# Banded attention in a hybrid mixer block: scores in passes of full height, values with the probabilities stationary

## The chip, the core and the metric

The kernel runs on one core of one Trainium2 chip. The metric is the device time of one execution in microseconds. A profile of one execution gives every instruction's start and duration on the engines: TensorE (PE for matmuls, PEld for the loads of the stationary operand), VectorE (DVE), ScalarE (ACT), GpSimd (POOL) and the DMA queue of SyncE (SP).

## What is computed

The reference is one layer of a decoder block with five token mixers (A to E) over 1024 positions of width 1024. One projection feeds all five; each branch is gated by SiLU(z), projected back, weighted by a sigmoid gate and summed. The change concerns branch C alone, sliding-window attention with 8 query heads, 2 key/value heads, head size 64, a window of 128, a relative bias and learned sinks:

```python
def _swa_sinks(q, k, v, sinks, band_bias):
    ...
    kb, vb = band(k), band(v)          # block n sees blocks n-1 and n: 256 keys
    s = jnp.einsum('bniKgd,bnjKd->bnKgij', qb, kb).astype(jnp.float32) * (hd ** -0.5)
    s = s + band_bias.astype(jnp.float32).reshape(1, 1, HKV, G, W, 2 * W)
    ...
    m = jnp.maximum(jnp.max(s, axis=-1, keepdims=True), sink)
    p = jnp.exp(s - m)
    p = p / (jnp.sum(p, axis=-1, keepdims=True) + jnp.exp(sink - m))
    o = jnp.einsum('bnKgij,bnjKd->bniKgd', p.astype(v.dtype), vb)
    return o.reshape(B, S, HQ, hd)
```

## The kernel before

Almost all of the kernel's time goes into large projections. A projection unit loads 128 columns of weights (512 KB), splits them into a high part `wh` (rounded by ACT, L222) and a low part `wl` (the rest, by GpSimd, L223), and runs 48 matmuls of 512 columns in threes, high x high, high x low, low x high (`mm3`, L277 to L279). These are the background matmuls of this text.

The branches' own work is written as Python generators. Each `tick()` in a projection unit, after every second k, so after six background matmuls, resumes the generators of the moment for one step. That sets the order in which instructions are emitted; a scheduler then orders them on each engine, and each engine runs its list strictly in order.

`attn_c` is such a generator. It runs under `m_units(3)`, twelve units of two gates and one branch projection in turn, and ends in the units of `z_units("cz", ...)`, whose `finish` needs the branch's output. It has 32 tasks: 8 blocks of 128 queries (`n`), two key/value heads (`g`), two pairs of query heads (`ip`). Step `i` of its loop has three parts with a tick between each: the scores of task i (`scores`), the values of task i-2 if it closes a head group (`values`), the transposes of task i-1 (`trans`).

- `split(n)` cuts the queries of a block: the 64 rows of the own half of `q` hold the rounded queries (ACT, L1394), the other 64 rows the rest (DVE, L1395). `ck_fn` does the same for the keys: `kk[g]` holds the rounded keys in both halves, `kl` the rest.
- `scores`: per head one matmul on all 128 rows (L1406), which gives (rounded + rest of q) x rounded k, and one on the 64 rows of one half (L1407), rounded q x rest of k. DVE scales and adds the bias out of PSUM (L1411), takes the maximum (L1414 to L1417); ACT makes exp and the row sums (L1419, L1421); DVE adds, inverts (L1422, L1423) and multiplies the probabilities with the inverse (L1425).
- `trans`: the probabilities are transposed on TensorE (L1437) and copied out of PSUM by ACT as `pT` (L1438).
- `values`: the values are the stationary operand, 128 keys x 64, and `pT` with 512 columns (4 heads x 128 queries) moves past it (L1448). The output stands with the head's 64 channels in partitions, each `g` in its half. ACT copies it to `yC` (L1451).

PSUM has two tiles of 512 columns for scores (`pa`), two (`pb`) for transposes and values, and two double ones (`mm`) for the background. The queries have three buffers, `p` two, `pT` one.

The branch projection of a unit ends in a product on DVE (L1029, out of PSUM) and a sum on GpSimd into `merged` (L1032).

Of the kernel before, what the change touches and what calls it, by code (L numbers as in the profile page):

```python
# [9 lines left out]
F32 = mybir.dt.float32  # L10
F32R = mybir.dt.float32r
AF = mybir.ActivationFunctionType
ALU = mybir.AluOpType
# [3 lines left out]
P = 128  # L17
T = 1024
# [113 lines left out]
def trunk(ctx, tc, a, out):  # L132
    nc = tc.nc
    act, dve, pool, pe, sp = nc.scalar, nc.vector, nc.gpsimd, nc.tensor, nc.sync

    def dump(name, ap):
        if name in a:
            sp.dma_start(a[name], ap)

    def open_pool(name, side="left", **kw):  # L140
        st = ExitStack()
        pl = st.enter_context(tc.tile_pool(name=name, bufs=1, side=side, reuse_waits="tile", **kw))
        return pl, st
# [11 lines left out]
    def nm(s):  # L155
        uid[0] += 1
        return f"{s}_{uid[0]}"

    def mm_t():
        return psm.tile([P, 2, 512], F32, name=nm("mm"), tag="mm")  # L160
# [17 lines left out]
    def pa_t():  # L178
        return pss["a"][0].tile([P, 512], F32, name=nm("pa"), tag="pa")

    def pb_t():
        return pss["b"][0].tile([P, 512], F32, name=nm("pb"), tag="pb")
# [8 lines left out]
    def bcol(*key):  # L191
        return col("b_in", _TIDX[key])

    ident = cst.tile([P, P], F32, name="ident")
# [23 lines left out]
    def f32(ap):  # L218
        return ap.bitcast(F32)
# [131 lines left out]
    def project(hi, lo):  # L351
        ps = mm_t()
        for hf in range(2):
            tl = slice(hf * 512, hf * 512 + 512)
            for k in range(8):
                wl_ = slice(k * P, (k + 1) * P)
                mm3(ps[:, hf, :], hi[:, wl_], lo[:, wl_], hTh[k][:, tl], hTl[k][:, tl], k == 0, k == 7)
                if k % 2:
                    tick()
        return ps  # L360

    units = []
    pools = {}
# [209 lines left out]
    def wait(n):  # L573
        for _ in range(n):
            yield
# [762 lines left out]
    def open_c():  # L1338
        st_["pd"].close()
        pc_, st_["pc"] = open_pool("pc", side="right")  # L1340
        pools["pc"] = pc_
        pools["yC"] = pc_.tile([P, 4, T], F32, name="yC")
        band = pc_.tile([P, 8, 256], F32, name="band")
        sp.dma_start(band, pools["band_src"])
        pools["band"] = band
        dump("dbg_band", band)
        pools["kk"] = [pc_.tile([P, T], F32R, name=f"kk{g}") for g in range(2)]
        pools["kl"] = pc_.tile([P, T], F32R, name="kl")
        pools["vt"] = pc_.tile([P, 8, P], F32, name="vt")
    ev(open_c)  # L1350

    def ck_fn(hi, lo):
        ps = project(hi, lo).rearrange("p a b -> p (a b)")
        b = bcol("ck", 0)

        for g in range(2):
            own, oth = slice(64 * g, 64 * g + 64), slice(64 - 64 * g, 128 - 64 * g)
            kk = pools["kk"][g]
            act.activation(kk[own], ps[own], AF.Identity, bias=b[own])
            dve.scalar_tensor_tensor(out=pools["kl"][own], in0=ps[own], scalar=b[own], in1=f32(kk[own]),  # L1360
                                     op0=ALU.add, op1=ALU.subtract)
            dve.tensor_copy(kk[oth], f32(kk[own]))

    def cv_fn(hi, lo):
        ps = project(hi, lo).rearrange("p a b -> p (a b)")
# [12 lines left out]

    def attn_c():
        pl = pools["pc"]  # L1380
        y, kk, kl, vt, band = (pools[k] for k in ("yC", "kk", "kl", "vt", "band"))
        tasks = [(n, g, ip) for n in range(8) for g in range(2) for ip in range(2)]
        qs, pts, pp, pos = {}, {}, {}, {}

        def dims(n):
            nk = 2 if n else 1
            return nk, ((n - 1) * P if n else 0), nk * P

        def split(n):
            for g in range(2):  # L1390
                q = pl.tile([P, 4, P], F32R, name=nm("q"), tag="q", bufs=3)
                own, oth = slice(64 * g, 64 * g + 64), slice(64 - 64 * g, 128 - 64 * g)
                src = y[own, :, n * P:(n + 1) * P]
                act.activation(q[own], src, AF.Copy)  # L1394
                dve.tensor_tensor(out=q[oth], in0=src, in1=f32(q[own]), op=ALU.subtract)  # L1395
                qs[n, g] = q

        def scores(n, g, ip):
            nk, k0, w = dims(n)
            q = qs[n, g]  # L1400
            r = slice(64 * g, 64 * g + 64)
            ps = pa_t()
            s3 = ps.rearrange("p (t m) -> p t m", t=2)[:, :, 0:w]
            for e in range(2):
                i = 2 * ip + e
                pe.matmul(s3[:, e, :], q[:, i, :], kk[g][:, k0:k0 + w], start=True, stop=False)  # L1406
                pe.matmul(s3[:, e, :], q[r, i, :], kl[r, k0:k0 + w], start=False, stop=True)  # L1407
            h0 = 4 * g + 2 * ip
            p = pl.tile([P, 2, 256], F32, name=nm("p"), tag="p", bufs=2)
            pv_ = p[:, :, 0:w]  # L1410
            dve.scalar_tensor_tensor(out=pv_, in0=s3, scalar=0.125, in1=band[:, h0:h0 + 2, 256 - w:256],  # L1411
                                     op0=ALU.mult, op1=ALU.add)
            mx = pl.tile([P, 8], F32, name=nm("mx"), tag="mx", bufs=4)
            dve.tensor_reduce(mx[:, 0:2], pv_, axis=AX.X, op=ALU.max)  # L1414
            dve.tensor_tensor(out=mx[:, 0:2], in0=mx[:, 0:2], in1=sinks[:, h0:h0 + 2], op=ALU.max)
            dve.tensor_tensor(out=mx[:, 2:4], in0=sinks[:, h0:h0 + 2], in1=mx[:, 0:2], op=ALU.subtract)
            dve.tensor_scalar_mul(mx[:, 0:2], mx[:, 0:2], -1.0)  # L1417
            for e in range(2):
                act.activation(pv_[:, e, :], pv_[:, e, :], AF.Exp, bias=mx[:, e:e + 1],  # L1419
                               accum_out=mx[:, 4 + e:5 + e])  # L1420
            act.activation(mx[:, 2:4], mx[:, 2:4], AF.Exp)  # L1421
            dve.tensor_tensor(out=mx[:, 4:6], in0=mx[:, 4:6], in1=mx[:, 2:4], op=ALU.add)  # L1422
            dve.reciprocal(mx[:, 4:6], mx[:, 4:6])  # L1423
            for e in range(2):
                dve.tensor_scalar_mul(pv_[:, e, :], pv_[:, e, :], mx[:, 4 + e:5 + e])  # L1425
            pp[n, g, ip] = p

        def trans(n, g, ip):
            nk, k0, w = dims(n)
            p = pp.pop((n, g, ip))  # L1430
            if ip == 0:
                pts[n, g] = pl.tile([P, 2, 512], F32, name=nm("pT"), tag="pT", bufs=1)
            pt = pb_t()
            pt4 = pt.rearrange("p (m t c) -> p m t c", m=2, t=2)
            for e in range(2):
                for m in range(nk):
                    pe.transpose(pt4[:, m, e, :], p[:, e, m * P:(m + 1) * P], ident)  # L1437
            act.activation(pts[n, g][:, 0:nk, ip * 256:ip * 256 + 256],  # L1438
                           pt.rearrange("p (m x) -> p m x", m=2)[:, 0:nk, :], AF.Copy)

        def values(n, g):
            nk, k0, w = dims(n)
            r = slice(64 * g, 64 * g + 64)
            if g == 0:
                pos[n] = pb_t()
            po = pos[n]
            for m in range(nk):
                pe.matmul(po[r, :], vt[:, k0 // P + m, r], pts[n, g][:, m, :], start=(m == 0), stop=(m == nk - 1),  # L1448
                          tile_position=(0, 64 * g))
            if g:  # L1450
                act.activation(y[:, :, n * P:(n + 1) * P], po.rearrange("p (i c) -> p i c", i=4), AF.Copy)  # L1451

        split(0)
        yield from wait(4)
        N = len(tasks)
        for i in range(N + 2):
            if i < N:
                scores(*tasks[i])
                if i % 4 == 1 and i + 3 < N:
                    split(tasks[i][0] + 1)  # L1460
            yield
            if i >= 2 and tasks[i - 2][2]:
                values(*tasks[i - 2][:2])
            yield
            if 1 <= i <= N:
                trans(*tasks[i - 1])
            yield
        marks.add("yC")
        dump("dbg_yC", y)

    start_bg("c", attn_c, 1.0)
    m_units(3, False)
    z_units("cz", 2, lambda t: pools["yC"][:, t, :], lambda t: "yC" in marks, "c")
# [51 lines left out]
    for t in range(8):  # L1525
# [6 lines left out]
        if t < 7:  # L1532
            ps = mm_t()
# [12 lines left out]
        n = len(parts)  # L1546
        for i, part in enumerate(parts):
            p, c0, w = part
# [42 lines left out]
```

## Time and profile before

| | us |
|---|---|
| median of 3 runs | 1709.17 (1707.18 to 1710.69) |
| the profiled execution | 1703.68 |
| its span, first to last instruction | 1701.9 |

| group in the attention stage (1204 to 1445 us) | count | busy us |
|---|---|---|
| background matmuls L277 to L279 | 609 | 262.2 summed |
| L1406, score pass on 128 rows (256 wide) | 56 | 15.7 |
| L1407, score pass on 64 rows (256 wide) | 56 | 21.3 |
| L1437, transposes of the probabilities | 120 | 32.5 |
| L1448, values, two records for each matmul | 60 | 34.8 |

The spans of matmuls overlap in the profile, so the busy times of the groups add up to more than the stage. What a matmul costs is read from the distance between starts. A row of the timeline reads: start in us, duration in us, engine, line, operation, output<-inputs by the program's names, tile shapes, count; and, in brackets, the idle time of the engine ahead of it with what ended that. A row of the groups reads: line, engine, operation, output<-inputs, shapes, count | busy us, mean ns of one | idle us just before them, and what ended it. `64*128` names the part of the array that a matmul uses: 64 rows, 128 columns.

### The profile page before, as it was taken

What the parts mean: (1) busy time and instruction counts of PE and PEld (TensorE: products, weight loads), DVE (VectorE), ACT (ScalarE), POOL (GpSimd) and SP (SyncE); (2) the same over time, 40 slices, a digit from 0 to 9 for tenths busy, and PEclk for the clock granted to TensorE, in tenths of its full rate; (3) what the DMA queues carried; (4) which work ended last, traced back from release to release, by engine and by line L of the source; (5) the groups of instructions that cost most, each with busy time, mean ns of one, the idle gap of its engine ahead of it and who ended that gap; (6) DMA issues with size and microseconds to landing.
All of it is one profiled execution on the core that took longest, in us unless ns stands there. A gap on an engine that the chain in (4) does not pass through costs nothing.

```text
span 1701.9 us, 18997 instructions
## 1 busy us (share of the span) xinstructions
PE 1644.6 (97%) x7634; PEld 1305.6 (77%) x7634; DVE 843.4 (50%) x1299; ACT 647.8 (38%) x1055; POOL 596.7 (35%) x315
## 2 busy tenths in 40 slices
PE   8989699999999998999999999999999999999998
PEld 7568588879788877888888777888765655888877
DVE  6678743485999873244546442210355544001712
ACT  6343223523421133435553566222544543212311
POOL 1454322432522249323344456552122212621121
PEclk9899799999999999999999999999999999999999
DMA  4111001110111111131111111121100001112322
GB/s 159 39 56 59 25 32 38 38 37 14 38 50 50 50 38 50 62 124 38 38 38 52 48 39 49 50 74 42 45 25 26 25 25 38 38 50 75 111 89 85
DMA packets 27128, 87.49 MB, mean 51 GB/s; under 512 B 5104, under 2 KB 6560, under 8 KB 26912
## 3 DMA queue, kind: packets, MB, share of 16 engines
q1 hardware_dynamic: 26896, 86.15, 15.8%
q8 instruction: 60, 0.98, 0.2%
q14 instruction: 28, 0.23, 0.0%
q10 hardware_dynamic: 144, 0.13, 0.0%
HBM read 82.06 MB, written 5.78 MB: 52 GB/s over the span
## 4 chain that ended last, share of the span: by engine, by line
PE 80%; DVE 13%; ACT 3%; POOL 2%; issue 1%; DMA 0%; SPq 0%; DVEq 0%; ACTq 0%; POOLq 0%
PE mm L278 22%; PE mm L277 22%; PE mm L279 22%; DVE qk L484 2%; PE pb L1448 2%; DVE lt L692 2%; DVE Ad L694 1%; PE pa L1407 1%; DVE v L484 1%; PE pb L722 1%; PE pa L722 1%; DVE m L612 1%; PE pb L1437 1%; PE pa L664 1%; DVE p L1183 1%
## 5 line engine op out<-in xcount | busy, mean ns | idle before, releaser
L277 PE MATMUL mm<-hTh,wh 128*128 128x512 f32 x1472 | 599.1, 407 | 0.0
L279 PE MATMUL mm<-hTh,wl 128*128 128x512 f32 x1472 | 588.3, 400 | 10.8 <-POOL wl L223 10.8
L278 PE MATMUL mm<-hTl,wh 128*128 128x512 f32 x1472 | 594.6, 404 | 0.0
L223 POOL TENSOR_TENSOR wl<-raw,wh 128x1024 fp32r<-128x1024 f32 x113 | 276.4, 2446 | 679.6 <-ACT wh L222 679.2
L277 PEld LDWEIGHTS mm<-hTh,wh 128*128 128x128 f32 x1472 | 279.3, 190 | 71.5 <-issue 10.8
L279 PEld LDWEIGHTS mm<-hTh,wl 128*128 128x128 f32 x1472 | 279.2, 190 | 69.5 <-POOL wl L223 12.0
L278 PEld LDWEIGHTS mm<-hTl,wh 128*128 128x128 f32 x1472 | 279.5, 190 | 68.4 <-issue 13.6
L222 ACT ACTIVATE wh<-raw 128x1024 fp32r<-128x1024 f32 (+1 forms) x131 | 129.9, 998 | 392.9 <-issue 237.7
L876 DVE SCALAR_TENSOR_TENSOR pc<-u,sm,pc 128x1024 f32<-128x1024 f32 x120 | 154.6, 1289 | 3.8
L277 PE MATMUL mm<-yh,wh 128*128 128x512 f32 x320 | 129.0, 403 | 0.0
L278 PE MATMUL mm<-yl,wh 128*128 128x512 f32 x320 | 128.8, 402 | 0.0
L279 PE MATMUL mm<-yh,wl 128*128 128x512 f32 x320 | 126.2, 395 | 0.0
L972 DVE SCALAR_TENSOR_TENSOR sg<-mm,sm,sg 128x1024 f32<-128x1024 f32 x20 | 25.7, 1283 | 126.6 <-ACT sg L971 100.8
L1032 POOL TENSOR_TENSOR merged<-merged,sg 128x1024 f32<-128x1024 f32 x24 | 58.9, 2455 | 58.7 <-DVE sg L1029 36.3
L277 PEld LDWEIGHTS mm<-yh,wh 128*128 128x128 f32 x320 | 60.1, 188 | 18.4 <-issue 3.2
L278 PEld LDWEIGHTS mm<-yl,wh 128*128 128x128 f32 x320 | 60.1, 188 | 17.1 <-issue 3.9
L279 PEld LDWEIGHTS mm<-yh,wl 128*128 128x128 f32 x320 | 60.1, 188 | 12.7
L1029 DVE TENSOR_TENSOR sg<-mm,sg 128x1024 f32<-128x1024 f32 x27 | 33.0, 1220 | 51.8 <-PE mm L279 34.2
L223 DVE TENSOR_TENSOR wol<-raw,woh 128x1024 fp32r<-128x1024 f32 x8 | 10.1, 1265 | 90.1 <-ACT woh L222 89.9
L1564 POOL TENSOR_TENSOR res<-res,xr 128x512 f32<-128x512 f32 x14 | 17.8, 1292 | 83.8 <-DVE res L1562 76.0
L1411 DVE SCALAR_TENSOR_TENSOR p<-pa,band 128x512 f32<-128x512 f32 (+1 forms) x32 | 21.0, 658 | 48.2 <-PE pa L1407 48.1
L279 PE MATMUL mm<-woh,ml 128*128 128x512 f32 x112 | 44.3, 395 | 0.0
(426 smaller groups left out, 2389.2 us busy)
## 6 DMA issues: line engine op xcount, KB each, us to landing
raw<-in_w_t SPq DMA_DIRECT2D x94, 512.0 KB, 3.5
raw<-in_w_br SPq DMA_DIRECT2D x20, 512.0 KB, 3.5
xt<-in_x SPq DMA_DIRECT2D x8, 512.0 KB, 8.7
raw<-in_w_mem SPq DMA_DIRECT2D x8, 512.0 KB, 3.6
raw<-in_w_out SPq DMA_DIRECT2D x8, 512.0 KB, 3.5
xr<-in_x SPq DMA_DIRECT2D x8, 512.0 KB, 5.1
out_dram<-res SPq DMA_DIRECT2D x7, 512.0 KB, 2.9
d_rt<-d_rb SPq DMA_DIRECT2D x1, 1536.0 KB, 8.0
```

The source lines that it names most:

```text
L222: act.activation(hi, raw, AF.Copy)
L223: eng.tensor_tensor(out=lo, in0=raw, in1=f32(hi), op=ALU.subtract)
L277: pe.matmul(o, lh, rh, start=start, stop=False)
L278: pe.matmul(o, lh, rl, start=False, stop=False)
L279: pe.matmul(o, ll, rh, start=False, stop=stop)
L484: dve.scalar_tensor_tensor(out=acc, in0=xp[:, j:j + 1024], scalar=cw(j), in1=acc, op0=ALU.mult, op1=ALU.add)
L692: dve.tensor_tensor(out=t3, in0=V3[:, 0:r, j:j + 1].broadcast_to([P, r, n]), in1=A3[:, j:j + 1, j + 1:32].broadcast_to([P, r, n]), op=ALU. ...
L722: pe.matmul(ps[:, j * P:(j + 1) * P], lhs[:, j, :], rhs[:, j, :], start=True, stop=True)
L876: dve.scalar_tensor_tensor(out=acc, in0=u[:, j:j + 1024], scalar=w(j), in1=acc, op0=ALU.mult, op1=ALU.add)
L1029: dve.tensor_tensor(out=(merged[d] if first else sgs[d])[:, cl], in0=p2, in1=sgs[d][:, cl], op=ALU.mult)
L1032: (dve if last else pool).tensor_tensor(out=merged[d][:, cl], in0=merged[d][:, cl], in1=sgs[d][:, cl], op=ALU.add)
L1448: pe.matmul(po[r, :], vt[:, k0 // P + m, r], pts[n, g][:, m, :], start=(m == 0), stop=(m == nk - 1), tile_position=(0, 64 * g))
```

## The change

Three things are done differently in `attn_c` and `ck_fn`.

The keys: `kk[g]` holds the rounded keys in one half and the rest in the other; `kl` is gone, and two copies with it. The queries: `qh` holds the rounded queries in both halves, `ql` the rest in both. Each head has two score passes, `qh` x `kk` and `ql` x `kk`, both on all 128 rows; the product of both rests comes along. ACT copies twice and DVE subtracts twice for each block and `g`; `qh` and `ql` have two buffers each.

The values: the slice of `pT` for one head (128 keys x 128 queries) is the stationary operand, and the 64 columns of `vt` move. The output has the queries in partitions, so the inverse of the row sum is a factor of a partition: the probabilities are not normalised any more, `rinv` keeps the inverses of a block, and DVE multiplies the output with them on its way from PSUM to `yC`.

The way back: a new function `back(n)` transposes the block of `yC` on TensorE, four 128 x 128, and ACT copies it back in place. It is called in the second part of step i = 4n + 6, one task step after the block's last values; the loop has one step more.

```diff
@@ ck_fn @@
-            dve.scalar_tensor_tensor(out=pools["kl"][own], in0=ps[own], scalar=b[own], in1=f32(kk[own]),
+            dve.scalar_tensor_tensor(out=kk[oth], in0=ps[own], scalar=b[own], in1=f32(kk[own]),
                                      op0=ALU.add, op1=ALU.subtract)
-            dve.tensor_copy(kk[oth], f32(kk[own]))
@@ split @@
-                q = pl.tile([P, 4, P], F32R, name=nm("q"), tag="q", bufs=3)
+                qh = pl.tile([P, 4, P], F32R, name=nm("qh"), tag="qh", bufs=2)
+                ql = pl.tile([P, 4, P], F32R, name=nm("ql"), tag="ql", bufs=2)
                 own, oth = slice(64 * g, 64 * g + 64), slice(64 - 64 * g, 128 - 64 * g)
                 src = y[own, :, n * P:(n + 1) * P]
-                act.activation(q[own], src, AF.Copy)
-                dve.tensor_tensor(out=q[oth], in0=src, in1=f32(q[own]), op=ALU.subtract)
-                qs[n, g] = q
+                act.activation(qh[own], src, AF.Copy)
+                act.activation(qh[oth], src, AF.Copy)
+                for r in (own, oth):
+                    dve.tensor_tensor(out=ql[r], in0=src, in1=f32(qh[own]), op=ALU.subtract)
+                qs[n, g] = qh, ql
@@ scores @@
-                pe.matmul(s3[:, e, :], q[:, i, :], kk[g][:, k0:k0 + w], start=True, stop=False)
-                pe.matmul(s3[:, e, :], q[r, i, :], kl[r, k0:k0 + w], start=False, stop=True)
+                for q in qs[n, g]:
+                    pe.matmul(s3[:, e, :], q[:, i, :], kk[g][:, k0:k0 + w], start=(q is qs[n, g][0]),
+                              stop=(q is qs[n, g][1]))
...
-            dve.reciprocal(mx[:, 4:6], mx[:, 4:6])
-            for e in range(2):
-                dve.tensor_scalar_mul(pv_[:, e, :], pv_[:, e, :], mx[:, 4 + e:5 + e])
+            if g == ip == 0:
+                rinv[n] = pl.tile([P, 8], F32, name=nm("rinv"), tag="rinv", bufs=3)
+            rv = rinv[n].rearrange("p (i g) -> p i g", g=2)
+            dve.reciprocal(rv[:, 2 * ip:2 * ip + 2, g], mx[:, 4:6])
@@ values @@
-            for m in range(nk):
-                pe.matmul(po[r, :], vt[:, k0 // P + m, r], pts[n, g][:, m, :], start=(m == 0), stop=(m == nk - 1),
-                          tile_position=(0, 64 * g))
+            po = pos[n].rearrange("p (i g c) -> p i g c", i=4, g=2)
+            for i in range(4):
+                for m in range(nk):
+                    pe.matmul(po[:, i, g, :], pts[n, g][:, m, i * P:(i + 1) * P],
+                              vt[:, k0 // P + m, 64 * g:64 * g + 64], start=(m == 0), stop=(m == nk - 1))
             if g:
-                act.activation(y[:, :, n * P:(n + 1) * P], po.rearrange("p (i c) -> p i c", i=4), AF.Copy)
+                dve.tensor_tensor(out=y[:, :, n * P:(n + 1) * P].rearrange("p i (g c) -> p i g c", g=2), in0=po,
+                                  in1=rinv[n].rearrange("p (i g) -> p i g", g=2).unsqueeze(3).broadcast_to([P, 4, 2, 64]),
+                                  op=ALU.mult)
+
+        def back(n):
+            pt = pb_t()
+            for i in range(4):
+                pe.transpose(pt[:, i * P:(i + 1) * P], y[:, i, n * P:(n + 1) * P], ident)
+            act.activation(y[:, :, n * P:(n + 1) * P], pt.rearrange("p (i c) -> p i c", i=4), AF.Copy)
...
-            if i >= 2 and tasks[i - 2][2]:
+            if 2 <= i < N + 2 and tasks[i - 2][2]:
                 values(*tasks[i - 2][:2])
+            if i >= 3 and i % 4 == 2:
+                back(tasks[i - 3][0])
```

How the instructions stand now. First TensorE, from the second head of task 13 (block 3) into the values of block 2's second head group; `pa` are scores, `pb` values, `mm` the background. Before:

```order
L1406 MATMUL pa_9035<-kk_8004,q_8850 128x256
L279 MATMUL mm_9062<-yh_7804,wl_8860 128x512
L1407 MATMUL pa_9035<-kl,q_8850 128x256
L277 MATMUL mm_9062<-yh_7867,wh_8859 128x512
L278 MATMUL mm_9062<-yl_7868,wh_8859 128x512
L279 MATMUL mm_9062<-yh_7867,wl_8860 128x512
L1448 MATMUL pb_8961<-pT_8970,vt 64x512
L277 MATMUL mm_9062<-yh_7930,wh_8859 128x512
L1448 MATMUL pb_8961<-pT_8970,vt 64x512
L278 MATMUL mm_9062<-yl_7931,wh_8859 128x512
```

The same place of the new kernel:

```order
L1407 MATMUL pa_9070<-kk_8004,qh_8866 128x256
L279 MATMUL mm_9101<-yh_7804,wl_8882 128x512
L1407 MATMUL pa_9070<-kk_8004,ql_8867 128x256
L277 MATMUL mm_9101<-yh_7867,wh_8881 128x512
L278 MATMUL mm_9101<-yl_7868,wh_8881 128x512
L279 MATMUL mm_9101<-yh_7867,wl_8882 128x512
L1451 MATMUL pb_8991<-vt,pT_9006 128x64
L277 MATMUL mm_9101<-yh_7930,wh_8881 128x512
L1451 MATMUL pb_8991<-vt,pT_9006 128x64
L278 MATMUL mm_9101<-yl_7931,wh_8881 128x512
L1451 MATMUL pb_8991<-vt,pT_9006 128x64
L279 MATMUL mm_9101<-yh_7930,wl_8882 128x512
```

The scores stand where they stood; the values go from two rows to eight, each between background matmuls.

Second TensorE again, one task step later, from the last score pass of task 14 over the end of a background unit (`yh` is its last input, `hTh` the first of the next). Before:

```order
L1407 MATMUL pa_9091<-kl,q_8853 128x256
L277 MATMUL mm_9062<-yh_7993,wh_8859 128x512
L278 MATMUL mm_9062<-yl_7994,wh_8859 128x512
L279 MATMUL mm_9062<-yh_7993,wl_8860 128x512
L277 MATMUL mm_9124<-hTh_101,wh_8980 128x512
L278 MATMUL mm_9124<-hTl_109,wh_8980 128x512
```

The same place of the new kernel, where `pb` and `yC` belong to `back`:

```order
L1407 MATMUL pa_9136<-kk_8005,ql_8873 128x256
L277 MATMUL mm_9101<-yh_7993,wh_8881 128x512
L278 MATMUL mm_9101<-yl_7994,wh_8881 128x512
L279 MATMUL mm_9101<-yh_7993,wl_8882 128x512
L1461 MATMUL pb_9159<-ident,yC 128x128 x2
L277 MATMUL mm_9173<-hTh_101,wh_9016 128x512
L1461 MATMUL pb_9159<-ident,yC 128x128
L278 MATMUL mm_9173<-hTl_109,wh_9016 128x512
L1461 MATMUL pb_9159<-ident,yC 128x128
```

The four transposes of block 2 have come in directly behind the unit's end.

Third DVE, the tail of task 9 (`p_8836` before, `p_8854` now) and the head of task 10. Before:

```order
L1417 TENSOR_SCALAR mx_8838<-mx_8838 128x2
L1422 TENSOR_TENSOR mx_8838<-mx_8838 128x2
L1411 SCALAR_TENSOR_TENSOR p_8898<-pa_8893,band 128x512
L1423 RECIPROCAL mx_8838<-mx_8838 128x2
L1414 TENSOR_REDUCE mx_8900<-p_8898 128x2
L1425 TENSOR_SCALAR p_8836<-p_8836,mx_8838 128x256 x2
L1395 TENSOR_TENSOR q_8853<-yC,q_8853 64x512
```

The same place of the new kernel; L1412 is what L1411 was, L1423 and L1427 what L1422 and L1423 were:

```order
L1418 TENSOR_SCALAR mx_8856<-mx_8856 128x2
L1454 TENSOR_TENSOR yC<-pb_8779,rinv_8614 128x4x128
L1423 TENSOR_TENSOR mx_8856<-mx_8856 128x2
L1427 RECIPROCAL rinv_8823<-mx_8856 128x2
L1397 TENSOR_TENSOR ql_8867<-yC,qh_8866 64x512 x2
L1412 SCALAR_TENSOR_TENSOR p_8926<-pa_8921,band 128x512
L1415 TENSOR_REDUCE mx_8928<-p_8926 128x2
```

The multiplications of the probabilities are gone; the scaling of block 1's values (L1454) and the two subtractions for task 12 (`ql_8867`) stand ahead of task 10's first operation.

More of the change, by code (lines that the diff above doesn't have):

```diff
@@ L1347, in open_c @@
         pools["kk"] = [pc_.tile([P, T], F32R, name=f"kk{g}") for g in range(2)]
-        pools["kl"] = pc_.tile([P, T], F32R, name="kl")
         pools["vt"] = pc_.tile([P, 8, P], F32, name="vt")
@@ L1380, in attn_c @@
         pl = pools["pc"]
-        y, kk, kl, vt, band = (pools[k] for k in ("yC", "kk", "kl", "vt", "band"))
+        y, kk, vt, band = (pools[k] for k in ("yC", "kk", "vt", "band"))
         tasks = [(n, g, ip) for n in range(8) for g in range(2) for ip in range(2)]
-        qs, pts, pp, pos = {}, {}, {}, {}
+        qs, pts, pp, pos, rinv = {}, {}, {}, {}, {}
         def dims(n):
@@ L1390, in split @@
             for g in range(2):
-                q = pl.tile([P, 4, P], F32R, name=nm("q"), tag="q", bufs=3)
+                qh = pl.tile([P, 4, P], F32R, name=nm("qh"), tag="qh", bufs=2)
+                ql = pl.tile([P, 4, P], F32R, name=nm("ql"), tag="ql", bufs=2)
                 own, oth = slice(64 * g, 64 * g + 64), slice(64 - 64 * g, 128 - 64 * g)
                 src = y[own, :, n * P:(n + 1) * P]
-                act.activation(q[own], src, AF.Copy)
-                dve.tensor_tensor(out=q[oth], in0=src, in1=f32(q[own]), op=ALU.subtract)
-                qs[n, g] = q
+                act.activation(qh[own], src, AF.Copy)
[3 more added lines that the diff above has]
+                qs[n, g] = qh, ql
         def scores(n, g, ip):
             nk, k0, w = dims(n)
-            q = qs[n, g]
-            r = slice(64 * g, 64 * g + 64)
             ps = pa_t()
@@ L1442, in values @@
             nk, k0, w = dims(n)
-            r = slice(64 * g, 64 * g + 64)
             if g == 0:
                 pos[n] = pb_t()
-            po = pos[n]
-            for m in range(nk):
-                pe.matmul(po[r, :], vt[:, k0 // P + m, r], pts[n, g][:, m, :], start=(m == 0), stop=(m == nk - 1),
-                          tile_position=(0, 64 * g))
-            if g:
-                act.activation(y[:, :, n * P:(n + 1) * P], po.rearrange("p (i c) -> p i c", i=4), AF.Copy)
+            po = pos[n].rearrange("p (i g c) -> p i g c", i=4, g=2)
[3 more added lines that the diff above has]
+                              vt[:, k0 // P + m, 64 * g:64 * g + 64], start=(m == 0), stop=(m == nk - 1))
+            if g:
+                dve.tensor_tensor(out=y[:, :, n * P:(n + 1) * P].rearrange("p i (g c) -> p i g c", g=2), in0=po,
[6 more added lines that the diff above has]
+            act.activation(y[:, :, n * P:(n + 1) * P], pt.rearrange("p (i c) -> p i c", i=4), AF.Copy)
         split(0)
@@ L1455, in attn_c @@
         N = len(tasks)
-        for i in range(N + 2):
+        for i in range(N + 3):
             if i < N:
```

## The prediction

> **What bounds the kernel now.** First the page's totals and its chain of waits, which say who is worth asking.
>
> ```profile
> PE 1644.6 (97%) x7634; PEld 1305.6 (77%) x7634; DVE 843.4 (50%) x1299; ACT 647.8 (38%) x1055; POOL 596.7 (35%) x315
> PE 80%; DVE 13%; ACT 3%; POOL 2%; issue 1%; DMA 0%; SPq 0%; DVEq 0%; ACTq 0%; POOLq 0%
> ```
>
> TensorE is busy 97% of the span and carries 80% of the chain that ends last. Next the busy times in three stretches (columns: PE, PEld, DVE, ACT, POOL, granted clock, DMA). The banded attention runs from 1204 to 1445 us.
>
> ```profile
> 238.00:260.00 22.00, 22.00 (x133) 19.38 (x132) 8.19 (x22) 8.16 (x26) 6.88 (x3) 1.00 0.08 25
> 1204.00:1445.00 241.00, 234.13 (x916) 148.44 (x916) 122.55 (x310) 114.28 (x252) 50.40 (x22) 0.98 0.09 28
> 1423.00:1433.00 10.00, 8.28 (x19) 3.29 (x17) 5.27 (x15) 3.07 (x11) 1.43 (x1) 0.66 0.14 52
> ```
>
> In that stage too TensorE is the bound: 234 of 241 us, with DVE and ACT half empty. So the change is worth what it does to the time of TensorE's own queue, plus what it does to the missing 7 us. Durations of single matmuls overlap in this profile (0.40 us each, though one starts every 0.23), so I price everything by **start-to-start times** in TensorE's timeline:
>
> ```profile
> 1303.49 0.28 PE L1406 MATMUL pa<-kk,q 128*128 128x256 f32 x1
> 1303.61 0.40 PE L277 MATMUL mm<-hTh,wh 128*128 128x512 f32 x1
> 1303.94 0.38 PE L1407 MATMUL pa<-kl,q 64*128 64x256 f32 x1
> 1304.25 0.50 PE L278 MATMUL mm<-hTl,wh 128*128 128x512 f32 x1
> 1304.58 0.28 PE L1406 MATMUL pa<-kk,q 128*128 128x256 f32 x1
> ...
> 1305.91 0.40 PE L279 MATMUL mm<-hTh,wl 128*128 128x512 f32 x1
> 1308.02 1.07 PE L1448 MATMUL pb<-pT,vt 128*64 128x512 f32 x2 [1.72 <-ACT pT L1438]
> 1309.02 0.49 PE L277 MATMUL mm<-hTh,wh 128*128 128x512 f32 x1
> 1309.45 1.07 PE L1448 MATMUL pb<-pT,vt 128*64 128x512 f32 x2
> 1310.45 0.50 PE L278 MATMUL mm<-hTl,wh 128*128 128x512 f32 x1
> 1310.78 0.39 PE L279 MATMUL mm<-hTh,wl 128*128 128x512 f32 x1
> 1311.01 0.40 PE L277 MATMUL mm<-hTh,wh 128*128 128x512 f32 x1
> ...
> 1311.72 0.27 PE L1437 MATMUL pb<-ident,p 128*128 128x128 f32 x1
> 1311.75 0.48 PE L277 MATMUL mm<-hTh,wh 128*128 128x512 f32 x1
> 1312.07 0.27 PE L1437 MATMUL pb<-ident,p 128*128 128x128 f32 x1
> ```
>
> The yardstick is the background matmul of 512 columns: 1310.78 to 1311.01, **0.23 us**. An inserted piece costs its period less 0.23 for each background matmul in it.
>
> **Part 1, the score passes.** One head (1303.49 to 1304.58) takes 1.09 us with two background matmuls in it, so its two passes cost 1.09 - 0.46 = 0.63 us. The pass on all 128 rows (L1406) takes only 0.12 of that (1303.49 to 1303.61). The pass on 64 rows (L1407) takes 0.31 itself, and makes the background matmuls on both sides 0.33 instead of 0.23. The weight-load rows say why:
>
> ```profile
> L1407 PEld LDWEIGHTS pa<-kl,q 64*128 64x128 f32 x64 | 11.7, 183 | 15.9 <-issue 15.9
> ...
> L1310 PEld LDWEIGHTS pa<-xs,wdl 64*128 64x128 f32 x16 | 2.9, 183 | 5.8 <-issue 5.8
> ```
>
> All 64 loads of half height are preceded by idle time of the loader (0.25 us each). So are the 16 of L1310, in another stage with other tiles. A load that changes the height is not started under the running matmul here, while full loads are. In the new kernel each head has two passes of the L1406 kind, 2 x 0.12 = 0.24. Saved: 0.63 - 0.24 = 0.39 us for each of 64 heads, 25.0; block 0 has passes of half the width with a little less to lose, so I take **-24.5 us**. The bounds are 0 (if the height is not the cause) and 25.
>
> The Trainium skill speaks against this gain: "TensorE: Matmul & The Clock Gate", section "Why this matters for your kernels", states that a matmul with a small K takes the same time as K=128, and Part 3 there that a load overlaps running matmuls only when its row group differs. By that rule the term would be 0 and the sum 24.5 us smaller. The trace disagrees in both points, with 0.31 against 0.12 us and a loader that idles only where the row group changes.
>
> **Part 2, the values.** Now 30 matmuls of 512 columns, each recorded twice (x2), into 64 columns of the array. Each takes 1.00 us (1308.02 to 1309.02), and the pair stretches its neighbours by 0.20 (0.43 between) and 0.10 (0.33 behind); at places without the wait 0.10 ahead as well. That is 2.4 us for two, 1.2 each, **36 us** for 30. In their place come 120 matmuls with a full 128 x 128 stationary and 64 columns moving. The trace has no such width, but the same type with 128 and with 32 columns:
>
> ```profile
> 240.50 0.38 PE L762 MATMUL pb<-S,qk 128*128 128x128 f32 x2
> 240.64 0.48 PE L278 MATMUL mm<-hTl,wh 128*128 128x512 f32 x1
> 240.96 0.38 PE L762 MATMUL pb<-S,qk 128*128 128x128 f32 x2
> ...
> 71.16 0.30 PE L438 MATMUL pa<-gdec,triu 128*128 128x32 f32 x2
> 71.30 0.39 PE L439 MATMUL pa<-gdec,ones 128*128 128x32 f32 x2
> ...
> 71.52 0.48 PE L278 MATMUL mm<-hTl,wh 128*128 128x512 f32 x1
> ...
> 71.84 0.39 PE L279 MATMUL mm<-hTh,wl 128*128 128x512 f32 x1
> ```
>
> 128 columns: 240.50 to 240.96, less 0.23 for L278, is 0.23. 32 columns: 71.16 to 71.84, less 0.23, is 0.45 for two, 0.225 each. The width does not matter; the two weight loads do. So 64 columns cost 0.225: 120 x 0.225 = 27 us. **-9 us**, between -8.4 (at 0.23) and, if each of four inner passes needed its own load, +18 (at 0.45).
>
> **Part 3, transposing back.** 32 more transposes of the L1437 kind: 1311.72 to 1312.07 is 0.35, less 0.23 is 0.12. **+3.8 us**, bounded by that and by the whole recorded 0.27 (8.7).
>
> The Trainium skill, "TensorE: Matmul & The Clock Gate", Part 4 ("PE-mode transpose"), gives about 275 ns for one in a kernel. By it the term would be 8.8 and the sum 5 us smaller. The recorded duration here, 0.27, is that number, but only 0.12 of it keeps the next instruction waiting.
>
> **Part 4, DVE and ACT.** Neither is the bound, so here only delays count.
>
> ```profile
> L1425 DVE TENSOR_SCALAR p<-p,mx 128x256 f32<-128x256 f32 x56 | 17.7, 358 | 0.8
> L1395 DVE TENSOR_TENSOR q<-yC,q 64x512 fp32r<-64x512 f32 x16 | 14.8, 922 | 52.3 <-ACT q L1394 51.8
> L1394 ACT ACTIVATE q<-yC 64x512 fp32r<-64x512 f32 x16 | 10.1, 628 | 10.5 <-PE pa L1407 10.4
> ```
>
> DVE loses the normalisation (17.7 us) and gains 16 more subtractions (at most 14.8) and 8 scalings out of PSUM, which I put between nothing and L1395's mean, 0.92 each (7.4 at most): within 5 us of even. ACT gains 16 copies, 10 us; its evacuation of the values gives way to one of the transposes, same shape. Both stay near 60% of the shortened stage. The order puts the new q halves two task steps ahead of the scores that read them, so the drop to two buffers costs nothing as long as those steps cover it. Those in the way of the scaled values are a transposition on TensorE and the evacuation in ACT's queue.
>
> **Part 5, the waits.** TensorE's own wait list has one entry here, and the chain of waits shows how it arises:
>
> ```profile
> PE pb L1448 <- ACT pT L1438: 6.9, 4, 1.7
> ```
> ```profile
> 1302.39 1.45 DVE mx L1415
> 1303.86 2.31 DVE mx L1416
> ...
> 1307.48 0.49 ACT pT L1438
> 1308.02 1.07 PE pb L1448 x2
> ```
> ```profile
> 1303.76 2.38 POOL L1032 TENSOR_TENSOR merged<-merged,sg 128x1024 f32<-128x1024 f32 x1
> ```
>
> Four times in the stage (odd blocks, first head group) two tiny DVE operations take 1.4 and 2.3 us; the second ends with GpSimd's sum into `merged` (1303.76 + 2.38 = 1306.14), so I read it as held up by that. exp and then pT wait behind them, and the values behind pT. All of that stays in its place and starts from the end of a background unit. TensorE however arrives earlier: between that end and the values it has 0.78 less of scores (two heads) and 0.46 more of transposes back. So each of the four waits grows by 0.32: **+1.3 us**. At the other sites pT is early:
>
> ```profile
> 1333.92 0.57 ACT L1438 ACTIVATE pT<-pb 128x512 f32<-128x512 f32 x1
> ...
> 1336.30 1.07 PE L1448 MATMUL pb<-pT,vt 128*64 128x512 f32 x2
> ```
>
> That is 1.8 us of cover (1334.49 to 1336.30), of which the change eats 0.3 to 0.8. If it were gone, a site would cost what exceeds it.
>
> **Sum.** -24.5 - 9.0 + 3.8 + 1.3 = **-28.4 us**. From the profiled span of 1701.9 that gives 1673.5, from that execution's own time (1703.68, 1.8 around the span) 1675.3. That execution lies 5.5 us below the median of the runs, 1709.17; the timed runs of the new kernel should lie by as much above theirs, so I take 1709.2 - 28.4 = **1681**.
>
> **The rivals.**
> - *New waits on the scaled values or on ql.* The transposes back need DVE's scaling, which stands in DVE's queue behind subtractions that GpSimd can stretch (L1395 averages 0.92). If each of the eight came late by one operation stretched like the 2.31 us above, that would take back 18: 1699. For: two more links on in-order engines. Against: about one task step of 6 us lies between values and transposes. 0.06.
> - *Full height is not what makes the pass cheap* (another operand, another accumulation order). Then part 1 is 0, the sum -3.9, the time 1705. Against: L1310 idles the loader in the same way with other operands and another shape. This is the skill's rule named above. 0.05.
> - *Slower: the clock.* The row from 1423 to 1433 has a granted clock of 0.66, just behind one of the four waits. The new values come in bursts of eight matmuls between eight background ones, 8 x 0.455 = 3.6 us, in which loads, not columns, set the pace. If that made the clock fall in each of the 16 bursts (14 of them full), each would take twice as long: 15 x 3.6 = +54, 1735. It decides from about eight bursts at half clock, which eat the whole gain. Against: the row from 238 to 260, full of the same pattern (L762), has clock 1.00. 0.05.
> - *The waits vanish* because the shortened softmax meets GpSimd at another moment: -9 more, 1672. For: such a meeting is a matter of a microsecond. Against: both ends hang on the same unit end. 0.06.
> - My forecast, 0.78.
>
> **How the numbers follow.** The stage's mean clock of 0.98 stands for some 5 us lost of 241; the new one can lose nothing or twice that; the offset between profile and timed runs is another 5. With the vanishing waits below and most of the new waits above, I take 1667 to 1698, which leaves out the two rivals at 1705 and 1735 and the last of the first. This kernel's runs can tell about 0.2% (3.4 us) from no change. Faster by more than that: 0.78 + 0.06 + 0.06 = 0.90. The 1705 case counts as within it: 0.05. Slower: 0.05.
>
> **What would show it.** Right: the half-height loads are gone from PEld and its "issue" idle with them; period of a head with two background matmuls 0.70 instead of 1.09; a value matmul between two background ones adds 0.23; the background work of those 241 us is done in about 213; DVE and ACT still under 65% there. Wrong: PE waits for DVE's scaled values or for ql; waits for pT at more than four sites; value matmuls that add 0.45; a granted clock below 0.9 in the stage.

## The result, and the profile after

| kernel | median us | lowest to highest | runs |
|---|---|---|---|
| before | 1709.41 | 1707.18 to 1710.69 | 4 |
| after | 1666.07 | 1665.65 to 1666.92 | 4 |

The ratio after to before is 0.9748, 95% interval 0.9732 to 0.9765: 43.3 us less, where 28 were forecast. The profiled execution of the new kernel took 1666.35 us with a span of 1664.6.

The page's totals and the engines of its chain, for the new kernel:

```profile
PE 1613.9 (97%) x7846; PEld 1327.6 (80%) x7846; DVE 842.4 (51%) x1257; ACT 655.0 (39%) x1071; POOL 596.7 (36%) x315
PE 80%; DVE 14%; ACT 3%; POOL 2%; issue 1%; DMA 0%; DVEq 0%; ACTq 0%; POOLq 0%
```

TensorE is the bound as before. Where the gain lies is told by two fixed points, the first score and the first operation of the final sum (a view of one line: count, shortest, median and longest ns, first and last start in us). Before:

```profile
L1406 PE MATMUL pa<-kk,q x64: 218/279/285, 1203.6 to 1422.9; 128*128 128x256 f32 x56, 128*128 128x128 f32 x8
...
L1562 DVE SCALAR_TENSOR_TENSOR res<-mm,rso,gpost x14: 740/746/751, 1620.4 to 1687.9; 128x512 f32<-128x512 f32 x14
```

After:

```profile
L1407 PE MATMUL pa<-kk,qh x64: 221/280/283, 1205.3 to 1391.0; 128*128 128x256 f32 x56, 128*128 128x128 f32 x8
...
L1575 DVE SCALAR_TENSOR_TENSOR res<-mm,rso,gpost x14: 742/748/753, 1583.0 to 1650.5; 128x512 f32<-128x512 f32 x14
```

From the one to the other it was 416.8 us and is 377.7: 39.1 less. The first point comes 1.7 later than before, and behind the second 81.5 and 81.6 us follow. So the whole difference of the two profiled spans (37.3) is made from the attention stage on.

The stage in the three-stretch view (columns: PE, PEld, DVE, ACT, POOL, granted clock, DMA):

```profile
1205.00:1412.00 207.00, 205.62 (x1149) 172.47 (x1148) 122.39 (x269) 121.00 (x267) 50.47 (x22) 1.00 0.11 34
```

TensorE idles 1.4 us here instead of 6.9, and its granted clock is 1.00, where the old kernel's row shows 0.98. DVE and ACT are 59% and 58% busy. Now TensorE's timeline, through the scores of two heads and the values of a head group at one of the four places where the old kernel waited:

```profile
1291.56 0.28 PE L1407 MATMUL pa<-kk,qh 128*128 128x256 f32 x1
1291.68 0.40 PE L277 MATMUL mm<-hTh,wh 128*128 128x512 f32 x1
1291.91 0.28 PE L1407 MATMUL pa<-kk,ql 128*128 128x256 f32 x1
1292.03 0.40 PE L278 MATMUL mm<-hTl,wh 128*128 128x512 f32 x1
1292.27 0.28 PE L1407 MATMUL pa<-kk,qh 128*128 128x256 f32 x1
...
1293.43 0.33 PE L1451 MATMUL pb<-vt,pT 128*128 128x64 f32 x2
1293.57 0.48 PE L277 MATMUL mm<-hTh,wh 128*128 128x512 f32 x1
1293.89 0.33 PE L1451 MATMUL pb<-vt,pT 128*128 128x64 f32 x2
...
1294.80 0.33 PE L1451 MATMUL pb<-vt,pT 128*128 128x64 f32 x2
1294.94 0.48 PE L277 MATMUL mm<-hTh,wh 128*128 128x512 f32 x1
1295.67 0.43 PE L1451 MATMUL pb<-vt,pT 128*128 128x64 f32 x2 [0.25 <-ACT pT L1440]
1295.91 0.48 PE L278 MATMUL mm<-hTl,wh 128*128 128x512 f32 x1
```

A head with two background matmuls takes 0.71 us (1291.56 to 1292.27), and no load of the second score pass is preceded by idle time of the loader any more, where the old L1407 had 15.9 us:

```profile
L1407 PEld LDWEIGHTS pa<-kk,ql 128*128 128x128 f32 x64 | 12.2, 190 | 0.0
```

A value matmul and a background one take 0.46 (1293.43 to 1293.89), 0.23 more than the background alone. And the wait for `pT` has moved: it stands ahead of the fifth value matmul, not the first. TensorE's wait list has that one entry (us in all, times, longest):

```profile
PE pb L1451 <- ACT pT L1440: 1.4, 4, 0.6
```

The idle time understates the cost, since matmul ends are modelled. By starts, L277 to the next L1451 takes 0.73 (1294.94 to 1295.67) where it is 0.32 without a wait; three places cost 0.41 so, the one at 1246.30 0.80 (its wait is 0.64 instead of 0.25), 2.0 in all. The same count of the old kernel gives 1.8 for each wait (1305.91 to 1308.02, less 0.33), 7.1 in all.

### The profile page after: what moved, and what is told of

The parts are those of the page before. It is cut to its first block, busy times and chain, and to the rows that moved or that the text cites. A ratio compares the mean times of both kernels' runs of the same rounds, so it can differ in the third digit from the quotient of the medians.

```text
span 1664.6 us, 19410 instructions
## 1 busy us (share of the span) xinstructions
PE 1613.9 (97%) x7846; PEld 1327.6 (80%) x7846; DVE 842.4 (51%) x1257; ACT 655.0 (39%) x1071; POOL 596.7 (36%) x315
## 3 DMA queue, kind: packets, MB, share of 16 engines
q1 hardware_dynamic: 26896, 86.15, 15.9%
## 4 chain that ended last, share of the span: by engine, by line
PE 80%; DVE 14%; ACT 3%; POOL 2%; issue 1%; DMA 0%; DVEq 0%; ACTq 0%; POOLq 0%
PE mm L278 22%; PE mm L277 22%; PE mm L279 22%; DVE qk L484 2%; DVE lt L692 2%; DVE Ad L694 1%; PE pb L1451 1%; DVE v L484 1%; PE pb L722 1%; PE pa L722 1%; PE pa L1407 1%; DVE m L612 1%; PE pb L1439 1%; PE pa L664 1%; DVE p L1183 1%
## 5 line engine op out<-in xcount | busy, mean ns | idle before, releaser
L277 PE MATMUL mm<-hTh,wh 128*128 128x512 f32 x1472 | 599.6, 407 | 0.0
L278 PE MATMUL mm<-hTl,wh 128*128 128x512 f32 x1472 | 594.1, 404 | 0.0
L277 PEld LDWEIGHTS mm<-hTh,wh 128*128 128x128 f32 x1472 | 279.5, 190 | 58.7 <-issue 0.2
L278 PEld LDWEIGHTS mm<-hTl,wh 128*128 128x128 f32 x1472 | 279.5, 190 | 55.1 <-issue 3.1
L277 PE MATMUL mm<-yh,wh 128*128 128x512 f32 x320 | 127.8, 399 | 0.0
L278 PE MATMUL mm<-yl,wh 128*128 128x512 f32 x320 | 127.4, 398 | 0.0
L277 PEld LDWEIGHTS mm<-yh,wh 128*128 128x128 f32 x320 | 60.1, 188 | 13.0 <-DVE sgl L1029 0.2
L278 PEld LDWEIGHTS mm<-yl,wh 128*128 128x128 f32 x320 | 60.2, 188 | 12.5 <-issue 1.5
L1397 DVE TENSOR_TENSOR ql<-yC,qh 64x512 fp32r<-64x512 f32 x32 | 27.6, 863 | 54.1 <-ACT qh L1394 53.7
L1451 PEld LDWEIGHTS pb<-vt,pT 128*128 128x128 f32 x240 | 43.2, 190 | 9.2 <-ACT pT L1440 2.6
```

The source lines that it names most:

```text
L277: pe.matmul(o, lh, rh, start=start, stop=False)
L278: pe.matmul(o, lh, rl, start=False, stop=False)
L1451: pe.matmul(po[:, i, g, :], pts[n, g][:, m, i * P:(i + 1) * P], vt[:, k0 // P + m, 64 * g:64 * g + 64], start=(m == 0), stop=(m == nk - 1))
```

## The experiments

All are compared with runs of the kernel before on the same chip: a median of 1707.09 (13 runs) beside the first four, 1706.08 (9 runs, 1698.06 to 1709.71) beside the others. The fastest runs of that kernel in the two comparisons, 1698.36 and 1698.06, agree, so times of different comparisons are set side by side below.

**The kernel before, unchanged**, to see what its own runs scatter by.

> The kernel before once more, unchanged, so that each timed run comes with its span and mean granted clock. Theory A (the waits and the half-clock spells behind them are part of what the change removed): the timed runs lie at 1707 to 1711 us with a mean clock below the 0.985 of the profiled execution of 1703.7, by about 0.003 for the missing 5.7 us, and any run near 1703 has 0.985 again. Theory B (the profile lies low for another reason): the clock of the timed runs is 0.985 within 0.001, whatever the time.

Ten runs: 1707.73, from 1698.32 to 1709.49, ratio 1.0002 (0.9982 to 1.0022). By and large the time goes with the mean granted clock: the run at 0.988 took 1698.3, the one at 0.987 1700.6, runs at 0.983 about 1707.7, runs at 0.982 up to 1709.5 (the one at 0.985, with 1707.4, is off this line). The new kernel's four runs stand at 0.988 to 0.989 and differ by 1.3 us. In the profiled run, windows around the first of the four waits, and the whole stage:

```profile
1246.00:1249.00 3.00, 1.79 (x7) 0.88 (x6) 1.81 (x2) 1.33 (x6) 1.62 (x1) 1.00 0.53 175
1249.00:1256.00 7.00, 6.50 (x10) 2.46 (x11) 4.35 (x14) 2.27 (x7) 0.00 (x0) 0.52 0.01 2
1256.00:1263.00 7.00, 7.00 (x34) 5.19 (x33) 1.87 (x5) 1.75 (x6) 0.00 (x0) 0.99 0.00 0
```
```profile
1204.00:1445.00 241.00, 234.14 (x902) 147.68 (x902) 121.30 (x309) 111.42 (x250) 47.56 (x21) 0.96 0.08 27
```

TensorE stands still from 1247.8 to 1249.5, and for 7 us around the end of that the clock is at 0.52: half speed for nearly all of it (7 x 0.48 / 0.5 = 6.7 us), 3.4 us lost, twice the wait itself. Behind each of the other three the clock falls as well, for a shorter or an equal time. Such stretches at half clock are called spells below. The stage's 0.96 stands for 241 x 0.04 = 9.6 us, and 1707.7 - 9.6 = 1698.1 is about what the fastest run takes. Runs like that one are called undisturbed below, as far as a clock of three digits can tell (0.001 of it is 1.7 us). So the median of the old kernel loses some 11 us to half clock (1709.4 - 1698.3), and its profiled run, with 0.98, about half of that.

**The second score pass on the 64 own rows**, all else as in the new kernel.

```diff
-                for q in qs[n, g]:
-                    pe.matmul(s3[:, e, :], q[:, i, :], kk[g][:, k0:k0 + w], ...)
+                qh, ql = qs[n, g]
+                r = slice(64 * g, 64 * g + 64)
+                pe.matmul(s3[:, e, :], qh[:, i, :], kk[g][:, k0:k0 + w], start=True, stop=False)
+                pe.matmul(s3[:, e, :], ql[r, i, :], kk[g][r, k0:k0 + w], start=False, stop=True)
```

> The new kernel with one thing undone: the second score pass runs on the 64 own rows of ql and kk alone, with the same operands, bank and width (it leaves out the product of the two rests). Theory A (the height of the load is what costs): about +24.5 us over the new kernel's 1666.1, so 1690 to 1691, and the loader idles 0.25 us ahead of all 64 half loads again, 16 us. Rival (another operand or accumulation order made the old pass dear): 1666, no idle ahead of the loads.

1687.01 (1686.03 to 1687.93), ratio 0.989 (0.9872 to 0.9908): 20.9 us more than the new kernel, where 24.5 were expected. Between the two fixed points of the profiled runs it is 399.2 (1203.9 to 1603.1) against 377.7, 21.5 more. The loader's idle time is back, with other operands than the old kernel had:

```profile
L1409 PEld LDWEIGHTS pa<-kk,ql 64*128 64x128 f32 x64 | 11.7, 183 | 15.7 <-issue 15.7
```
```profile
1294.07 0.28 PE L1408 MATMUL pa<-kk,qh 128*128 128x256 f32 x1
1294.19 0.39 PE L277 MATMUL mm<-yh,wh 128*128 128x512 f32 x1
1294.50 0.38 PE L1409 MATMUL pa<-kk,ql 64*128 64x256 f32 x1
1294.81 0.50 PE L278 MATMUL mm<-yl,wh 128*128 128x512 f32 x1
1295.15 0.28 PE L1408 MATMUL pa<-kk,qh 128*128 128x256 f32 x1
```

The head takes 1.08 us again, with L277 and L278 stretched to 0.31 and 0.34. Slower scores also leave `pT` more time: the four waits are gone, which hides 2.0 us. Passes of half height among full ones thus cost 20.9 + 2.0 = 22.9 us, 0.36 for a head (23.5 by the fixed points). Whether half height would cost as much where no load changes the height, no run shows.

**Heads 2 and 3 first in the values.** If the new order of the values is what covers the late copy, this must uncover it.

```diff
-            for i in range(4):
+            for i in (2, 3, 0, 1):
```

> The new kernel with the heads of a values group in the order 2, 3, 0, 1, the same work in the same places: the first matmuls of a group now need the later of the two copies of pT. Theory A (the waits shrank because heads 0 and 1 need only the early copy and cover the late one): the four waits move to the first matmul of a group and grow to 2.2 to 2.6 us each, 9 in all instead of 2, so +7 us, and half-clock spells may come back behind them, 0 to 10 more: 1673 to 1683. Theory B (they shrank because the softmax got shorter or meets GpSimd at another moment): 1666 within 1.

1674.59 (1673.27 to 1675.40), ratio 0.9819 (0.9798 to 0.9840): 8.5 us more, for the same instructions.

```profile
PE pb L1451 <- ACT pT L1440: 8.6, 4, 2.4
```

The waits went from 1.4 to 8.6 us. They are longer than the old kernel's 1.72, 2.06 at three of the four places, since TensorE comes earlier; 1.72 + 0.32 = 2.04 is what I had forecast for the new kernel itself. Behind one of them the profiled run has half clock, for 8 x 0.21 / 0.5 = 3.4 us:

```profile
1244.00:1252.00 8.00, 7.52 (x37) 6.59 (x38) 3.77 (x11) 3.58 (x9) 0.00 (x0) 0.79 0.01 2
```

**The new scores alone**, with the keys and queries that they need, put into the old kernel (values and normalisation stay old, and there is no way back). The diff shows the passes only.

```diff
...
-                pe.matmul(s3[:, e, :], q[:, i, :], kk[g][:, k0:k0 + w], start=True, stop=False)
-                pe.matmul(s3[:, e, :], q[r, i, :], kl[r, k0:k0 + w], start=False, stop=True)
+                for q in qs[n, g]:
+                    pe.matmul(s3[:, e, :], q[:, i, :], kk[g][:, k0:k0 + w], start=(q is qs[n, g][0]),
+                              stop=(q is qs[n, g][1]))
```

> The kernel before with the keys, queries and score passes of the new one, values and normalisation as before. Theory A: -24.5 us of TensorE time; the four waits for pT stay and grow by 0.78 each, 3.1 us, since TensorE comes earlier; half-clock spells stay: 1685 to 1691 timed (1709.4 - 21.4 and what the spells do), waits of about 10 us in all. Theory B (the score passes alone were priced too low, and the rest of the change brings what was forecast): -33 us or more, 1676 or less.

1688.35 (1686.92 to 1689.92), ratio 0.9898 (0.9879 to 0.9917), at a clock of 0.984 in all four runs. The time is inside the expectation, but not by the waits I had in mind:

```profile
PE pb L1438 <- DVE p L1426: 10.5, 7, 1.8
PE pb L1449 <- ACT pT L1439: 2.5, 1, 2.5
```
```profile
1237.90 1.22 DVE L1029 TENSOR_TENSOR sg<-mm,sg 128x1024 f32<-128x1024 f32 x1
1239.05 4.61 DVE L1426 TENSOR_SCALAR p<-p,mx 128x256 f32<-128x256 f32 x2
1243.58 0.67 DVE L1415 TENSOR_REDUCE mx<-p 128x2 f32<-128x512 f32 x1
```
```profile
1244.00:1252.00 8.00, 8.00 (x21) 4.48 (x21) 4.53 (x15) 3.45 (x10) 0.00 (x0) 0.64 0.00 1
```

The transposes now wait for the normalised probabilities: two multiplications of 0.36 each take 4.61 us together when they fall behind the end of a unit, where GpSimd works, and the clock falls behind that too. With the shortened scores another DVE operation has come into that place. In the new kernel this operation does not exist.

**The new values alone**, put into the old kernel, with the scaling and the way back; the scores stay old. The diff shows the value matmuls only.

```diff
...
-                pe.matmul(po[r, :], vt[:, k0 // P + m, r], pts[n, g][:, m, :], ...)
+                    pe.matmul(po[:, i, g, :], pts[n, g][:, m, i * P:(i + 1) * P],
+                              vt[:, k0 // P + m, 64 * g:64 * g + 64], start=(m == 0), stop=(m == nk - 1))
```

> The kernel before with the values, the normalisation and the way back of the new one; keys, queries and score passes as before. Theory A: -9 us for the values, +3.8 for the way back, -7 because heads 0 and 1 cover the late copy of pT (the four waits fall from about 1.8 us each to none or a few tenths), and no half-clock spells behind them: span 1696.6 (the runs before without a spell) - 12 = about 1685, time 1686 to 1688, all runs within 2 us of each other and the clock 0.988. Theory B (the waits only fell because the score passes changed): waits of 7 to 10 us remain, spells too: 1693 to 1705.

1686.35 (1686.00 to 1687.92), ratio 0.9891 (0.9859 to 0.9923). TensorE's wait list is empty in the stage, and the clock is whole:

```profile
1204.00:1430.00 226.00, 226.00 (x1136) 174.04 (x1136) 109.76 (x254) 113.69 (x251) 49.88 (x21) 1.00 0.09 31
```

Against the undisturbed runs of the kernel before (1698.3) that is 12 us less. The waits that are gone cost 7.1, which leaves 4.9 for values and way back, where 9.0 - 3.8 = 5.2 were forecast. Against its median beside (1706.1) it is 20.

**The old values, six background matmuls later**, so that the late copy is covered; nothing else is changed in the old kernel.

```diff
             yield
+            yield
             if i >= 2 and tasks[i - 2][2]:
                 values(*tasks[i - 2][:2])
-            yield
```

> The kernel before with one thing moved: the values of a group are issued six background matmuls later, ahead of the transposes; no work added or taken away. Theory A (each of the four waits brings half-clock spells with it): the waits fall from 1.8 us to about 0.4 each, the spells go, so the runs gather at 1693 to 1695 instead of 1698 to 1710, clock 0.988. Theory B (the spells come from the thin use of the array by the old values, whatever they wait for): the waits go, -6 us, but the spells and the scatter of 10 us stay, with a median near 1702.

1694.01 (1692.63 to 1696.09, 6 runs), ratio 0.9943 (0.9918 to 0.9968), at a clock of 0.988 to 0.989 in every run.

```profile
PE pb L1448 <- ACT pT L1438: 1.4, 4, 0.4
```
```profile
1204.00:1445.00 241.00, 239.60 (x961) 155.35 (x960) 123.43 (x310) 117.04 (x255) 55.93 (x24) 1.00 0.09 29
```

The same instructions, with 5.5 us less of idle time, take 12 to 13 less than the medians of the kernel before: the spells go with the waits. The scatter of 11.7 us beside it shrinks to 3.5.

**Full height in another branch.** The idle time at L1310 has the same cause if the cure works there. The pass becomes one on all 128 rows, and the product of both rests comes along.

```diff
-                    pe.matmul(ps, wdl[own, n, :], x2[own, sl], start=False, stop=True)
+                    pe.matmul(ps, wdl[:, n, :], x2[:, sl], start=False, stop=True)
```

> The new kernel with the same cure in branch D: its 16 second passes on 64 rows (512 columns) become passes on all 128 rows, whose stationary operand stands in both halves already (the product of the two rests comes along). If height is what costs, 16 x 0.39 = 6.2 us, or 5.8 by what half heights cost in the new kernel: 1660. If not, 1666.

1658.97 (1658.11 to 1659.28), ratio 0.9728 (0.9697 to 0.9759): 7.1 us less than the new kernel, where 5.8 to 6.2 were expected. Not all of that is the height: the profiled run starts its first L1309, just ahead of the first changed pass, at 951.1 instead of 952.0. From there to the last L1309, at 1046.9 instead of 1053.6, lie fifteen of the changed passes; this takes 95.8 us instead of 101.6, 0.39 less for each. The matmul of that line went from a median of 494 ns to 388, and no idle time stands before its loads any more:

```profile
L1310 PE MATMUL pa<-xs,wdl x16: 388/388/392, 951.5 to 1047.3; 128*128 128x512 f32 x16
```

**Both, and the values in halves**: heads 0 and 1 in their place, heads 2 and 3 one tick later.

```diff
             if 2 <= i < N + 2 and tasks[i - 2][2]:
-                values(*tasks[i - 2][:2])
+                values(*tasks[i - 2][:2], (0, 1))
...
             yield
+            if 2 <= i < N + 2 and tasks[i - 2][2]:
+                values(*tasks[i - 2][:2], (2, 3))
             if 1 <= i <= N:
                 trans(*tasks[i - 1])
```

> lru_full, with the values of a group in two halves: heads 0 and 1 where they stand, heads 2 and 3 six background matmuls later, ahead of the transposes. Theory A: the last 2 us of waits for pT go as well, 1658. Rival: the transposes come later by the second half, so the copy of pT behind them does too, and a wait comes back at the next group: 1660 or more.

1656.81 (1655.22 to 1657.17), ratio 0.9717 (0.9680 to 0.9754), less than the kernels before and after. One wait of 0.4 us is left:

```profile
PE pb L1450 <- ACT pT L1440: 0.4, 1, 0.4
```

## Why the prediction was off

Compared at full clock the change is worth 1698.3 - 1666.1 = 32.2 us; another 11 are half clock that went with the waits. The lower end of the range, 1667, is the rival of the vanishing waits (1672) with 5 us of clock; the waits did shrink, and the clock gave twice that. The steps in turn:

- **Part 1, the scores: right in cause, a little too large.** Height is what makes the pass dear: undoing it alone brought back the idle loader and 22.9 us (23.5 between the fixed points). From the other side, 1686.35 with the new values and old scores to 1666.07 is 20.3, plus 2.0 for the waits that come back, 22.3 (again 399.2 against 377.7 and 23.5 between the fixed points, 1203.8 to 1603.0). So the term is -22 to -23.5, not -24.5, and the rival by which height is not the cause is out. One reading went too far: the loader does not idle only where the row group changes. In the old kernel 19 of the 60 loads of L1448, on all 128 rows but 64 columns, have 5.4 us of the same idle time. The Trainium skill's rule that a small K takes as long as K=128 ("TensorE: Matmul & The Clock Gate", "Why this matters for your kernels") does not hold here in a stream of full passes, by these runs and by the 0.39 us for each pass of L1310.
- **Parts 2 and 3, values and way back: right.** 0.23 for a value matmul was read off the timeline, and for the two together the run of the new values alone leaves -4.9, where -5.2 was forecast. No term depended on the width of 64.
- **Part 4: right.** DVE stayed even (843.4 us in all before, 842.4 after). The stage's rows for the subtractions and the scalings show DVE's two new loads. TensorE's wait list names neither `ql` nor `yC`, so the first rival did not occur:

```profile
L1397 DVE TENSOR_TENSOR ql<-yC,qh 64x512 fp32r<-64x512 f32 x28 | 24.2, 865 | 1.6 <-ACT qh L1394 1.2
...
L1454 DVE TENSOR_TENSOR yC<-pb,rinv 128x512 f32<-128x512 f32 x8 | 5.5, 684 | 5.1 <-PE pb L1451 5.1
```

- **Part 5, the waits: wrong in sign.** The step that failed is "So each of the four waits grows by 0.32". It took the wait as one in front of the whole head group. The old value matmul has all 512 columns of `pT` as its input, so it does need the late copy. The new one needs 128 columns, and the columns of heads 0 and 1 were copied one task earlier. Four value matmuls with their background ones, 1.8 us, now run while ACT makes the late copy. The chain of waits of the new kernel shows that the copy itself is as late as it ever was:

```profile
1289.39 0.60 DVE mx L1415
1290.01 1.45 DVE mx L1416
1291.49 2.33 DVE mx L1417
1293.84 0.20 ACT mx L1422
1294.04 1.09 ACT p L1420 x4
1295.14 0.49 ACT pT L1440
1295.67 0.43 PE pb L1451 x2
```

  It ends 2.2 us behind the first value matmul (1293.43), and 1.8 of that are covered. Turning the heads round took the cover away and gave the longer waits that I had forecast. The term is 2.0 - 7.1 = -5.1 instead of +1.3. The rival of the vanishing waits had the direction, not the reason: DVE's 1.45 and 2.33 us are still there, and the second still ends with GpSimd's sum into `merged`, the first with the split of weights ahead of it:

```profile
1289.03 2.40 POOL L223 TENSOR_TENSOR wl<-raw,wh 128x1024 fp32r<-128x1024 f32 x1 [6.02 <-ACT wh L222]
1291.39 2.40 POOL L1032 TENSOR_TENSOR merged<-merged,sg 128x1024 f32<-128x1024 f32 x1
```

  The Trainium skill ("SBUF — State Buffer", "Who interferes with whom") states that a DVE operation with two inputs in SBUF contends with a GpSimd one that reads it. The trace agrees: L1416 and L1417 have two and take 1.45 and 2.33 us; L1415 ahead of them has one and takes 0.60, beside the same GpSimd split; the median of the 32 executions of each of L1416 and L1417 is 0.16. That GpSimd is the cause was not tried by itself.
- **The sum: wrong in its base.** The step is "the timed runs of the new kernel should lie by as much above theirs". The 5.5 us between the profiled run and the median were half-clock spells behind the four waits, so they went with the waits, as did those that the profiled run itself had. I had seen one spell (0.66 from 1423 to 1433, just behind a wait) and held it for a risk of the new bursts, not for a price of the old waits. The clock rival thus pointed the wrong way: the bursts of value matmuls run at a granted clock of 1.00.

The account at full clock: scores -22.5, values -9.0, way back +3.8, waits -5.1, together -32.8, against 32.2 measured. Between the fixed points, where differences ahead of the stage do not enter, the old kernel's two profiled runs less their half clock take 416.8 - 5.1 = 411.7 and 420.9 - 10.2 = 410.7 (its spells are 6.83, 3.41, 3.41 and 6.83 us long) against 377.7: 33 to 34, and with 23.5 for the scores the account says 33.8. The forecast of -28.4 differs from -43.3 by 11 for the clock and 6.4 for the waits, less 2.0 for the scores and about half a microsecond that is not told apart.

## What to carry to other kernels

Ask of every wait which part of its input is late, and whether the new order of work needs that part first: splitting two matmuls into eight moved the wait behind 1.8 us of useful work. When a kernel's runs scatter by several microseconds and the granted clock goes with them, find the waits that stand ahead of the spells and price them with the spell; moving the values by six matmuls was worth 12 us of the median here, for 5.5 of idle time. In a stream of full-height matmuls with large background work, a second pass of half height costs more than one of full height, so fill the idle rows with something harmless.

## What the hardware showed unexpectedly

- The granted clock halves for 3.4 or 6.8 us behind waits of TensorE of only 1.7 us, behind two to four of the four waits in the profiled runs of the kernel before. The two spells of its first profiled run, each as a window of its own (granted clock 0.50):

```profile
1367.84:1371.26 3.42, 3.42 (x7) 1.52 (x7) 2.06 (x8) 1.30 (x5) 0.00 (x0) 0.50 0.00 0
1425.87:1432.70 6.83, 6.39 (x9) 2.36 (x10) 3.60 (x13) 1.68 (x6) 0.00 (x0) 0.50 0.00 0
```

  The Trainium skill ("TensorE: Matmul & The Clock Gate", "Why this matters for your kernels") speaks of gaps of over about 3 us; the trace has them behind 1.7. Waits of 0.25 to 0.64 us (the new kernel) have none behind them.
- Whether a wait has a spell behind it goes with where it falls in time. The starts of the two spells above lie 58.03 us apart, 17 x 3.413, and in all ten traces every change of the granted clock lies on such a grid of 3.41 us. The grid lies differently against the kernel's start from run to run: the last line before the first wait is at 1244.96 in one profiled run of the old kernel and at 1245.84 in the other. The old kernel's two runs and the one with heads 2 and 3 first have twelve waits of 1.7 to 2.4 us. In the seven with a spell behind them at least 1.2 us of the wait lay ahead of the next line, and the spell starts at that line. In the five without, at most 0.7 us lay ahead of it, and the 1.3 to 1.6 us of the wait behind the line brought none. So the scatter of the old kernel's runs is chance in where the grid lies, as far as twelve waits tell; nothing was moved to try it, and why 1.2 us of idle time ahead of a line is enough stays open. The Trainium skill ("TensorE: Matmul & The Clock Gate", Part 1, "The HAM clock gate") says that the activity window of about 3.4 us runs free of the kernel's start; the traces agree, with the grid of 3.41 us above.
- One load of half height among full ones is preceded by 0.25 us of idle time of the loader with 256 columns moving (L1407) and 0.36 with 512 (L1310, 5.8 us for 16); the pass costs 0.36 us more than a full one in the first case and 0.39 in the second.
